# Key and query latents normed for all tokens at once, with the norm weights applied after the transposes, in a hybrid SSM and attention block

## The chip, the cores and the metric

The kernel runs on one core of a Trainium2 chip. The metric is device time in microseconds (us), the median of three runs. One further execution was recorded by the hardware profiler; every row shown here is from that execution.

## What is computed

One layer of a streaming encoder for 512 tokens of width 1024, all in float32. The part that the change touches is the projection of the normed input and the latent attention that follows it:

```python
h = rmsnorm(x, norm_mix_w)
u_ssd, u_mla = jnp.split(h @ w_in, [IN_SSD], axis=-1)
# u_ssd: gates z (1024), x (1024), B (512), C (512), dt (16)
y_ssd = ssd_mixer(u_ssd, ...)      # conv, SiLU, chunked scan, gate, grouped norm
q_lat, kv_lat, k_rope = jnp.split(u_mla, [384, 384 + 256], axis=-1)   # k_rope: 32
q  = rmsnorm(q_lat, q_norm_w) @ w_q_up        # 16 heads of 64 + 32
kv = rmsnorm(kv_lat, kv_norm_w) @ w_kv_up     # 16 heads of 64 + 64
# rotary embedding on q's last 32 columns and on k_rope, scale 96 ** -0.5,
# softmax over blocks of the past, y_mla = p @ v
x = x + concat([y_ssd, y_mla]) @ w_out
...  # memory attention, conv FFN, final norm
```

## The kernel before

Tokens stand in four tiles of 128 (`t` is a tile). A product in float32 is made of three matmuls on split operands (`mm3`, lines L103 to L105): each number is a high part (ScalarE, written ACT in the profile, copies it in a rounded type: L94, or with a scale per partition L98) and a low part (VectorE, written DVE, subtracts: L95, L99). Activations are split once. Weights come in **pages** (`wr`) of 128 partitions by 1024 numbers, loaded by SyncE's queue (SP) into three buffers and split into `wh` and `wl`, four buffers each. For each page ACT casts, then DVE subtracts (L95, whole page); while the flag `pool_helps` is set, DVE takes half (L157) and GpSimd (POOL) the other half (L158). The flag is set from the tenth of 16 steps of the state-space scan to the end of the memory attention.

The scan goes over four groups of heads with four chunks each. In groups 0 to 2 each step runs, ahead of its chunk, a **unit** of the next group's projections on TensorE (PE): B, C or one of two x units (`acc<-wh,Ah`, 24 matmuls of 256 or 512 columns), and a gate unit (`z_unit`), then `ssd_d`, `ssd_a`, `ssd_b` (the scan itself). An x unit is evicted through a convolution: ACT `cu`, three DVE passes (L434), DVE `cu` (L437), and four transposes (`tr<-cst,cu`). Group 3 has no next group; the table `PLAN` writes out what its four steps run. Its letters: `z` a gate unit; `l` a **late unit**, the last 432 of the latents' columns for one token tile (24 matmuls of 432 columns, four pages of 2x432); `d`, `a`, `b` the scan; `i` sets up tiles and weights of the latent norm; `q0` to `q3` and `k0` to `k3` norm the query and the key latents of one token tile; `p1` runs one out-projection part (`out_part`, 12 matmuls of 256 columns); `U` the first query up-projection (`q_up`, its rotary work on POOL, L726 to L729), `s` and `S` the setup of the key and query tiles.

`lat_norm` does per token tile: squares on ACT, mean and epsilon on DVE (`msl`, L140), the power -1/2 on POOL (`rsl`, L142), a multiplication by that and the weight row on DVE (L621), two or three transposes on PE (`tr<-cst,qkl`), and the splits on ACT and DVE for each 128x128 block (`lt`, L94, L95). `lat_kv` also turns `k_rope` on DVE (L635 to L638).

After group 3 comes the attention; it takes the remaining out parts, the second half of the out projection and the memory keys as fills, one or two a head. Memory attention and the feed-forward follow.

A scheduler orders each engine's queue from the program's text and its own estimates (except where `manual_schedule` fixes the first norm), and each engine works its queue strictly in order: an instruction that waits holds what stands behind it. At the start DVE and PE norm the token tiles one after the other: `ms` (L140), `xn` (L287), four transposes, the splits `Al`.

Of the kernel before, what the change touches and what calls it, by code (L numbers as in the profile page):

```python
# [7 lines left out]
F32 = mybir.dt.float32  # L8
# [6 lines left out]
P = 128  # L15
T = 512
# [17 lines left out]

PLAN = ('z z z z d a l l b', 'l l d a i q0 k0 p1 q1 b p1 q2 k1 p1 q3 k2', 'p1 d a k3 p1 b p1', 'p1 d U p2 b p3 s S')


def shape_constants():
    t = np.arange(P)[:, None]
    l = np.arange(P)[None, :]  # L40
    cen = ((t > 63) & (t <= l)).astype(np.float32) - ((t > l) & (t <= 63))
    c = np.concatenate([t == l, t <= l, cen, t <= l, t > l, np.ones((P, P))], axis=1).astype(np.float32)
    m = np.zeros((NT, 2, T), np.float32)
    for j in range(NT):
        m[j, 0, j * P:j * P + 64] = 1.0
        m[j, 1, j * P + 64:(j + 1) * P] = MASK_NEG
    f = np.array([np.float32(1.0) / np.float32(np.float64(10000.0) ** np.float64(np.float32(i) / np.float32(ROPE)))
                  for i in range(0, ROPE, 2)], np.float32).reshape(1, ROPE // 2)
    return c, m, f
# [13 lines left out]
def tile_block(ctx, tc, x, mem, positions, norm_mix_w, w_in, ssd_conv_w, ssd_conv_b, ssd_dt_bias,  # L63
# [80 lines left out]

    pool_helps = [False]
    def wload(src, a, b):
# [3 lines left out]

    def wsplit(raw, pool=False):
        _, a, b = raw.shape
        hi = base.tile([P, a, b], F32R, name="wh", tag="wh", bufs=4)
        lo = base.tile([P, a, b], F32R, name="wl", tag="wl", bufs=4)
        if pool or (pool_helps[0] and a > 1):
            nc.scalar.copy(hi, raw)  # L156
            nc.vector.tensor_tensor(lo[:, 0:a // 2], raw[:, 0:a // 2], f32(hi[:, 0:a // 2]), ALU.subtract)  # L157
            nc.gpsimd.tensor_tensor(lo[:, a // 2:], raw[:, a // 2:], f32(hi[:, a // 2:]), ALU.subtract)  # L158
        else:
            split(hi, lo, raw)  # L160
# [100 lines left out]
    ones = k1([1, P], "ones")  # L261
    nc.vector.memset(ones, 1.0)
    scb = base.tile([P, 16], F32, name="scb")
    drow = base.tile([P, SSD_H], F32, name="drow")
# [150 lines left out]
    nc.vector.tensor_copy(cosb[:, :, H2:], cosb[:, :, 0:H2])  # L415
    nc.vector.tensor_scalar(sinb[:, :, 0:H2], sinb[:, :, H2:], -1.0, None, ALU.mult)


# [186 lines left out]
    def lat_init():  # L605
        LT.extend(k4([P, 2, T], "lt", F32R) for _ in range(3))
        LT.extend(page("lt") for _ in range(2))
        qkl = k4([P, 1024], "qkl")
        box["qw"], box["kvw"] = row_tile(qkl[:, 0:QR], mla_q_norm_w), row_tile(qkl[:, QR:QR + KVR], mla_kv_norm_w)
        box["ln"] = qkl[:, QR + KVR:]  # L610
        nc.vector.tensor_scalar(box["qw"], box["qw"], float(QH) ** -0.5, None, ALU.mult)
        x4 = k4([P, 4, 256], "xo")
        xo.extend(x4[:, i] for i in range(3))
        box["lnk"] = [gw[0], x4[:, 3]]

    def lat_norm(t, o, n, w, l0, l1, ln):
        ss = small([P, 1], "ssl", 2)
        src = lat[:, t, SSD_H + o:SSD_H + o + n]
        nc.scalar.activation(ln, src, AF.Square, accum_out=ss)
        rs = rstd_of(ss, n, "l")  # L620
        nc.vector.scalar_tensor_tensor(ln, src, rs, w, ALU.mult, ALU.mult)  # L621
        ps = tr_bank().rearrange("p (k t) -> p k t", k=4)
        for k in range(l0, l1):
            transpose(ps[:, k - l0], ln[:, tsl(k - l0)])
        for k in range(l0, l1):
            split(LT[k][:, 0, tsl(t)], LT[k][:, 1, tsl(t)], ps[:, k - l0])

    def lat_q(t):
        lat_norm(t, 0, QR, box["qw"], 0, 3, box["ln"])

    def lat_kv(t):
        lat_norm(t, QR, KVR, box["kvw"], 3, 5, box["lnk"][t % 2])
        kr = lat[:, t, SSD_H + QR + KVR:]
        tmp = small([P, ROPE], "krt", 1)
        nc.vector.tensor_tensor(tmp[:, 0:H2], kr[:, H2:], sinb[:, t, 0:H2], ALU.mult)  # L635
        nc.vector.tensor_tensor(tmp[:, H2:], kr[:, 0:H2], sinb[:, t, H2:], ALU.mult)
        nc.vector.tensor_tensor(kr, kr, cosb[:, t], ALU.mult)
        nc.vector.tensor_tensor(kr, kr, tmp, ALU.add)  # L638

    with tc.issue_after(last):  # L640
# [24 lines left out]
    def late_unit(t):  # L665
# [5 lines left out]
        for k in range(KD):  # L671
            hi, lo = late_pages[k // 2]
            mm3(acc, (hT[0][:, k, tsl(t)], hT[1][:, k, tsl(t)]), (hi[:, k % 2], lo[:, k % 2]), k == 0, k == KD - 1)
        nc.scalar.copy(lat[:, t, 256:], acc)

    late = [lambda t=t: late_unit(t) for t in range(NT)]
# [8 lines left out]
    def setup_kq1():  # L685
        for b in range(2):
            kt = k4([P, 2, T], f"kt{b}", F32R)
            qt = k4([P, 2, T], f"qt{b}", F32R)
            for i, (tl, w) in enumerate(((qt, masks[:, 0]), (kt, masks[:, 1]))):
                nc.vector.memset(f32(tl[QH:KROWS, 1]), 0.0)  # L690
                nc.gpsimd.dma_start(tl[QH:KROWS, 0], w)
            kts.append(kt)
# [144 lines left out]
    def do(op, i):  # L837
# [11 lines left out]
        elif op == "i":  # L849
            lat_init()  # L850
        elif op[0] == "q":
            lat_q(int(op[1]))
        elif op[0] == "k":
            lat_kv(int(op[1]))
        elif op[0] == "p":
# [9 lines left out]
    for i, (g, c) in enumerate(seq):  # L865
        pool_helps[0] = i > 9
        if g + 1 < SSD_G:
# [180 lines left out]
    with tc.manual_schedule(engines={E_.PE, E_.Activation, E_.DVE}):  # L1048
# [47 lines left out]
        for n0 in (0, 256):  # L1096
            for m in range(2):
                fm_pass(accs0[m], pg0, m, h3t, n0, n0 + 256)
            if n0 == 0:
                scaled(3)  # L1100
                turn(3)
                store(3)
    pool_helps[0] = False
    acts = []
# [122 lines left out]
```

## Time and profile before

| | us |
|---|---|
| median of three runs | 987.85 (987.63 to 988.17) |
| the profiled execution, its own time | 987.27 |
| its span in the trace | 985.5 |
| PE busy in the span | 965.7 (98%) |
| DVE, ACT, POOL busy | 662.1 (67%), 523.4 (53%), 279.6 (28%) |

The span is what the trace covers; 1.8 us of the execution lie outside it. Busy times are sums over instructions of an engine; PE is the only engine near its span, so a time is read as PE's work plus the pauses in which PE waited.

### The profile page before, as it was taken

What the parts mean: (1) busy time and instruction counts of PE and PEld (TensorE: products, weight loads), DVE (VectorE), ACT (ScalarE), POOL (GpSimd) and SP (SyncE); (2) the same over time, 40 slices, a digit from 0 to 9 for tenths busy, and PEclk for the clock granted to TensorE, in tenths of its full rate; (3) what the DMA queues carried; (4) which work ended last, traced back from release to release, by engine and by line L of the source; (5) the groups of instructions that cost most, each with busy time, mean ns of one, the idle gap of its engine ahead of it and who ended that gap; (6) DMA issues with size and microseconds to landing.
All of it is one profiled execution on the core that took longest, in us unless ns stands there. A gap on an engine that the chain in (4) does not pass through costs nothing.

```text
span 985.5 us, 14980 instructions
## 1 busy us (share of the span) xinstructions
PE 965.7 (98%) x5385; PEld 843.0 (86%) x5385; DVE 662.1 (67%) x1210; ACT 523.4 (53%) x1078; POOL 279.6 (28%) x360
## 2 busy tenths in 40 slices
PE   8999999999999999999999999999999999999997
PEld 6889998898899999988888888888888888888886
DVE  5989999868779786773654435766667666722553
ACT  5677776655477677753544434444444444321442
POOL 2016547656653547452443222000000000000000
PEclk9999999999999999999999999999999999999999
DMA  7653432315423336242241120433223322332462
GB/s 242 208 175 95 116 108 77 97 49 179 155 78 103 113 113 233 86 155 80 86 150 65 65 86 22 128 107 107 86 87 108 105 85 93 113 116 97 156 223 80
DMA packets 90306, 114.07 MB, mean 116 GB/s; under 512 B 5799, under 2 KB 70119, under 8 KB 89848
## 3 DMA queue, kind: packets, MB, share of 16 engines
q1 hardware_dynamic: 88536, 106.78, 34.0%
q0 software_dynamic: 1696, 6.33, 2.1%
q8 instruction: 43, 0.70, 0.3%
q14 instruction: 31, 0.25, 0.1%
HBM read 104.67 MB, written 8.42 MB: 115 GB/s over the span
## 4 chain that ended last, share of the span: by engine, by line
PE 82%; DVE 7%; DMA 3%; ACT 3%; POOL 2%; issue 2%; SPq 0%; POOLq 0%; ACTq 0%; DVEq 0%
PE acc L103 22%; PE acc L105 22%; PE acc L104 22%; PE tr L119 3%; PE s L103 3%; PE s L105 3%; PE s L104 3%; PE pv L811 2%; DMA aE<-acT 2%; DVE wl L157 1%; ACT aE L544 1%; PE acc L119 1%; DVE cu L434 1%; DMA wr<-in_w_in_dram 1%; POOL xdD L550 1%
## 5 line engine op out<-in xcount | busy, mean ns | idle before, releaser
L103 PE MATMUL acc<-Ah,wh 128*128 128x512 f32 (+1 forms) x560 | 215.5, 385 | 0.2 <-ACT Ah L94 0.2
L104 PE MATMUL acc<-Al,wh 128*128 128x512 f32 (+1 forms) x560 | 215.4, 385 | 0.2 <-DVE Al L95 0.2
L105 PE MATMUL acc<-Ah,wl 128*128 128x512 f32 (+1 forms) x560 | 215.0, 384 | 0.0
L95 DVE TENSOR_TENSOR wl<-wr,wh 128x1024 fp32r<-128x1024 f32 (+1 forms) x99 | 120.0, 1213 | 101.6 <-ACT wh L94 100.9
L94 ACT CAST wh<-wr 128x1024 fp32r<-128x1024 f32 (+1 forms) x99 | 102.0, 1031 | 133.5 <-PE acc L104 63.7
L158 POOL TENSOR_TENSOR wl<-wr,wh 128x512 fp32r<-128x512 f32 (+2 forms) x64 | 103.5, 1625 | 86.2 <-ACT wh L156 79.8
L142 POOL TENSOR_TENSOR rs<-ms,neg_half 128x1 f32<-128x1 f32 x18 | 10.8, 600 | 409.5 <-DVE ms L140 397.9
L104 PEld LDWEIGHTS acc<-Al,wh 128*128 128x128 f32 x560 | 105.3, 188 | 20.3 <-DVE Al L95 0.5
L105 PEld LDWEIGHTS acc<-Ah,wl 128*128 128x128 f32 x560 | 105.3, 188 | 20.2
L103 PEld LDWEIGHTS acc<-Ah,wh 128*128 128x128 f32 x560 | 105.2, 188 | 20.0 <-ACT Ah L94 0.5
L156 ACT CAST wh<-wr 128x1024 fp32r<-128x1024 f32 (+2 forms) x64 | 65.4, 1029 | 40.1 <-PE s L105 10.7
L1121 DVE SCALAR_TENSOR_TENSOR cbuf<-acc,fcw,cbuf 128x511 f32<-128x511 f32 (+1 forms) x88 | 65.6, 747 | 26.6 <-ACT cbuf L1119 25.1
L157 DVE TENSOR_TENSOR wl<-wr,wh 128x512 fp32r<-128x512 f32 (+2 forms) x64 | 59.3, 932 | 35.7 <-ACT wh L156 34.7
L103 PE MATMUL acc<-wh,Ah 128*128 128x256 f32 (+2 forms) x240 | 77.2, 323 | 1.0 <-ACT Ah L94 1.0
L105 PE MATMUL acc<-wh,Al 128*128 128x256 f32 (+2 forms) x240 | 76.2, 319 | 0.0
L104 PE MATMUL acc<-wl,Ah 128*128 128x256 f32 (+2 forms) x240 | 75.9, 318 | 0.0
L795 POOL TENSOR_SCALAR p<-p,ri 128x128 f32<-128x128 f32 (+1 forms) x64 | 34.5, 542 | 71.7 <-DVE ri L794 71.1
L103 PEld LDWEIGHTS acc<-wh,Ah 128*128 128x128 f32 x240 | 46.1, 192 | 4.2 <-ACT Ah L94 1.4
L105 PEld LDWEIGHTS acc<-wh,Al 128*128 128x128 f32 x240 | 46.1, 192 | 2.6 <-DVE Al L95 0.3
L104 PEld LDWEIGHTS acc<-wl,Ah 128*128 128x128 f32 x240 | 46.2, 192 | 2.3
L1119 ACT ACTIVATE cbuf<-acc,fcb,fcw 128x512 f32<-128x512 f32 x44 | 34.3, 779 | 24.0 <-PE acc L105 24.0
L104 PE MATMUL acc<-wl,act 128*128 128x512 f32 (+1 forms) x112 | 40.5, 363 | 0.0
(370 smaller groups left out, 2349.3 us busy)
## 6 DMA issues: line engine op xcount, KB each, us to landing
wr<-in_w_ffn_up_dram SPq DMA_DIRECT2D x44, 512.0 KB, 3.5
wr<-in_w_ffn_down_dram SPq DMA_DIRECT2D x33, 512.0 KB, 3.3
wr<-in_w_in_dram SPq DMA_DIRECT2D x26, 512.0 KB, 3.9
wr<-in_w_out_dram SPq DMA_DIRECT2D x16, 512.0 KB, 3.5
aE<-acT POOLq DMA_DIRECT2D x16, 256.0 KB, 3.5
wr<-in_w_mem_k_dram SPq DMA_DIRECT2D x8, 512.0 KB, 4.5
wr<-in_w_mem_v_dram SPq DMA_DIRECT2D x8, 512.0 KB, 3.4
wr<-in_w_mem_q_dram SPq DMA_DIRECT2D x8, 512.0 KB, 3.6
```

Source lines behind the costliest of these rows:

```text
L94: first = nc.scalar.copy(hi, src)
L95: nc.vector.tensor_tensor(lo, src, f32(hi), ALU.subtract)
L103: nc.tensor.matmul(acc, lhsT=lh, rhs=rh, start=first, stop=False)
L104: nc.tensor.matmul(acc, lhsT=lh, rhs=rl, start=False, stop=False)
L105: nc.tensor.matmul(acc, lhsT=ll, rhs=rh, start=False, stop=last)
L119: nc.tensor.transpose(dst, src, ident[:n, :n])
L156: nc.scalar.copy(hi, raw)
L157: nc.vector.tensor_tensor(lo[:, 0:a // 2], raw[:, 0:a // 2], f32(hi[:, 0:a // 2]), ALU.subtract)
L158: nc.gpsimd.tensor_tensor(lo[:, a // 2:], raw[:, a // 2:], f32(hi[:, a // 2:]), ALU.subtract)
L795: nc.gpsimd.tensor_scalar(p_, p_, ri, 1.0, ALU.mult, ALU.mult)
L1119: nc.scalar.activation(u, acc, AF.Identity, scale=fcw[:, 2, m:m + 1], bias=fcb[:, m:m + 1])
L1121: nc.vector.scalar_tensor_tensor(u[:, s:], acc[:, :T - s], fcw[:, 2 - s, m:m + 1], u[:, s:], ALU.mult, ALU.add)
```

## The change

The norm of the latents is done once for all four token tiles (`n`): squares on ACT behind each late unit, one power on POOL for 128x8 sums, eight scalings on ACT in place, rotary work on DVE for all tiles at once. The norm weights are no longer rows that DVE multiplies by; they are loaded as columns (`latw`, weight by partition) and applied where the transposes are split (`t0` to `t4`, one bank of four transposes each). In group 3 the late units come first and the gate units after them; out parts in group 3 are ten instead of twelve. Weight pages, apart from the first two, are no longer halved with POOL. The mask tiles are loaded whole instead of half loaded and half set to zero. A DMA scratch size is set.

```diff
-PLAN = ('z z z z d a l l b', 'l l d a i q0 k0 p1 q1 b p1 q2 k1 p1 q3 k2', 'p1 d a k3 p1 b p1', 'p1 d U p2 b p3 s S')
+PLAN = ('d a l l l l n z b z', 'z z d a i b p1 t0 p1 t1', 'd a p1 t2 t3 b p1 t4 p1', 'd U p2 b p3 s S')
...
-    m = np.zeros((NT, 2, T), np.float32)
+    m = np.zeros((NT, 2, 2, T), np.float32)
...
-    def wsplit(raw, pool=False):
+    def wsplit(raw, halves=False):
...
-        if pool or (pool_helps[0] and a > 1):
+        if halves:
...
+    latw = base.tile([P, 64], F32, name="latw")
...
+    nc.sync.dma_start(latw[:, 0:3], mla_q_norm_w[0].rearrange("(k p) -> p k", p=P))
+    nc.sync.dma_start(latw[:, 3:5], mla_kv_norm_w[0].rearrange("(k p) -> p k", p=P))
+    nc.vector.tensor_scalar(latw[:, 0:3], latw[:, 0:3], float(QH) ** -0.5, None, ALU.mult)
...
-        qkl = k4([P, 1024], "qkl")
-        box["qw"], box["kvw"] = row_tile(qkl[:, 0:QR], mla_q_norm_w), row_tile(qkl[:, QR:QR + KVR], mla_kv_norm_w)
...
-        nc.scalar.activation(ln, src, AF.Square, accum_out=ss)
-        rs = rstd_of(ss, n, "l")
-        nc.vector.scalar_tensor_tensor(ln, src, rs, w, ALU.mult, ALU.mult)
...
-            split(LT[k][:, 0, tsl(t)], LT[k][:, 1, tsl(t)], ps[:, k - l0])
...
+    def lat_norm():
...
+        rs = small([P, 2 * NT], "lrs", 1)
+        for i, n in enumerate((QR, KVR)):
+            h = slice(i * NT, (i + 1) * NT)
+            nc.vector.tensor_scalar(lss[:, h], lss[:, h], 1.0 / n, EPS, ALU.mult, ALU.add)
+        nc.gpsimd.tensor_tensor(rs, lss, neg_half.broadcast_to([P, 2 * NT]), ALU.pow)
+        for t in range(NT):
+            for i, (o, n) in enumerate(((SSD_H, QR), (SSD_H + QR, KVR))):
+                v = lat[:, t, o:o + n]
+                nc.scalar.activation(v, v, AF.Copy, scale=rs[:, i * NT + t:i * NT + t + 1])
+        kr = lat[:, :, SSD_H + QR + KVR:]
+        tmp = small([P, NT, ROPE], "krt", 1)
+        nc.vector.tensor_tensor(tmp[:, :, 0:H2], kr[:, :, H2:], sinb[:, :, 0:H2], ALU.mult)
...
+    def lat_T(k):
+        ps = tr_bank()
+        for t in range(NT):
+            transpose(ps[:, tsl(t)], lat[:, t, SSD_H + P * k:SSD_H + P * (k + 1)])
+        split(LT[k][:, 0], LT[k][:, 1], ps, latw[:, k:k + 1])
...
+        for i, (o, m) in enumerate(((SSD_H, QR), (SSD_H + QR, KVR))):
+            nc.scalar.activation(acc[:, 0:m], lat[:, t, o:o + m], AF.Square, accum_out=lss[:, i * NT + t:i * NT + t + 1])
...
-            for i, (tl, w) in enumerate(((qt, masks[:, 0]), (kt, masks[:, 1]))):
-                nc.vector.memset(f32(tl[QH:KROWS, 1]), 0.0)
-                nc.gpsimd.dma_start(tl[QH:KROWS, 0], w)
+            for i, tl in enumerate((qt, kt)):
+                nc.gpsimd.dma_start(tl[QH:KROWS], masks[:, i])
...
-        pool_helps[0] = i > 9
...
-    nc = _bacc.Bacc("TRN2", target_bir_lowering=False, num_devices=1)
+    nc = _bacc.Bacc("TRN2", target_bir_lowering=False, num_devices=1, dynamic_dma_scratch_size=8192)
```

Three places of the queues, before and now. First, DVE at the start of the program, where the second and third token tiles are normed (`ms`, `xn`). Before:

```order
L157 TENSOR_TENSOR wl<-wr,wh 128x512 x2
L95 TENSOR_TENSOR Al<-tr,Ah 128x4x128 x2
L140 TENSOR_SCALAR ms<-ss 128x1 x2
L287 SCALAR_TENSOR_TENSOR xn<-x,rs,s 128x512 x2
L95 TENSOR_TENSOR Al<-pv,Ah 128x4x128
```

Now:

```order
L156 TENSOR_TENSOR wl<-wr,wh 128x512 x2
L95 TENSOR_TENSOR Al<-tr,Ah 128x4x128 x2
L140 TENSOR_SCALAR ms<-ss 128x1
L421 TENSOR_SCALAR latw<-latw 128x3
L140 TENSOR_SCALAR ms<-ss 128x1
L287 SCALAR_TENSOR_TENSOR xn<-x,rs,s 128x512 x2
```

The scaling of the latent weights, which stands far down in the text, is queued between two steps of the first norm, and waits there for a load. That load's place in SP's queue now:

```order
L259 DMA cst<-in_consts_dram 128x128
L319 DMA drow<-in_ssd_d_dram 128x16
L419 DMA latw<-in_mla_q_norm_w_dram 128x3x1
L420 DMA latw<-in_mla_kv_norm_w_dram 128x2x1
L147 DMA wr<-in_w_in_dram 128x8x128
```

It stands right behind `drow` and ahead of the first page of the B unit, which followed `drow` before.

Second, POOL at the end of the scan, around the latent norm's power (`rsl`; `rsy` and `y` belong to the scan's own norm, `qrow` and `rt` to the queries' rotary work). Before:

```order
L142 TENSOR_TENSOR rsl<-msl,neg_half 128x1 x2
L593 TENSOR_TENSOR y<-y,gw 128x256
L142 TENSOR_TENSOR rsy<-msy,neg_half 128x1
L726 TENSOR_TENSOR rt<-qrow,sinb 128x4x16
L727 TENSOR_TENSOR rt<-qrow,sinb 128x4x16
L593 TENSOR_TENSOR y<-y,gw 128x256
L728 TENSOR_TENSOR qrow<-qrow,cosb 128x4x32
L567 TENSOR_TENSOR xdD<-xdD,y_478 128x256
L729 TENSOR_TENSOR qrow<-qrow,rt 128x4x32
L142 TENSOR_TENSOR rsl<-msl,neg_half 128x1 x2
```

Now, where the one power (`lrs`) stands:

```order
L555 TENSOR_TENSOR xdD<-xrow,dt 128x256
L556 TENSOR_TENSOR xdD<-xdD,dec 128x256
L581 TENSOR_TENSOR S<-S,dec 128x256
L624 TENSOR_TENSOR lrs<-lss,neg_half 128x8
L555 TENSOR_TENSOR xdD<-xrow,dt 128x256
```

The power has moved from behind the queries' rotary work to a place ahead of the last three chunks' outputs, and the rotary work now follows everything of the scan.

Third, DVE around the last x unit (group 3's second, whose convolution is L434 before, L439 now) and the late pages (`wl` 128x432 halves before, 128x864 whole now). Before:

```order
L95 TENSOR_TENSOR M<-aE,M 128x512
L586 TENSOR_TENSOR y<-pv,xdD 128x256
L157 TENSOR_TENSOR wl<-wr,wh 128x512
L577 TENSOR_TENSOR S<-s,S 128x256
L587 TENSOR_TENSOR y<-pv,y 128x256
L588 SCALAR_TENSOR_TENSOR y<-y,zrow 128x256
L95 TENSOR_TENSOR S<-S 128x256
L140 TENSOR_SCALAR msy<-ssy 128x1
L157 TENSOR_TENSOR wl<-wr,wh 128x512
L434 SCALAR_TENSOR_TENSOR cu<-acc,scw,cu 128x511
```

Now, the second, third and fourth late pages with what stands between them:

```order
L95 TENSOR_TENSOR wl<-wr,wh 128x864
L439 SCALAR_TENSOR_TENSOR cu<-acc,scw,cu 128x511
L140 TENSOR_SCALAR msy<-ssy 128x1
L439 SCALAR_TENSOR_TENSOR cu<-acc,scw,cu 128x510
L546 TENSOR_TENSOR cbm<-s,cst 128x128
L439 SCALAR_TENSOR_TENSOR cu<-acc,scw,cu 128x509
L95 TENSOR_TENSOR Bl<-tr,Bh 128x2x128
L551 TENSOR_TENSOR aE<-aE,cbm 128x512
L571 TENSOR_TENSOR y_482<-s,dec 128x256
L95 TENSOR_TENSOR wl<-wr,wh 128x864
L524 SCALAR_TENSOR_TENSOR zrow<-zrow,acc 128x256
L95 TENSOR_TENSOR wl<-wr,wh 128x864
```

Ahead of the first of these rows stand, in order, the first late page, `M`, `S`, two `y`, `S` and `y` of the scan. The late pages have moved ahead, between the last two chunks of group 2.

## Rows read from the trace of the kernel before

**Rows 1.** Windows: start to end, length, then busy time (count) of each engine, PE clock, DMA.

```profile
0.00:20.00 20.00, 15.08 (x73) 11.54 (x74) 9.41 (x20) 11.34 (x20) 5.96 (x10) 1.00 0.87 276
...
180.00:260.00 80.00, 73.76 (x493) 69.68 (x493) 60.56 (x143) 44.68 (x118) 52.83 (x70) 0.96 0.38 117
260.00:480.00 220.00, 219.67 (x1447) 202.28 (x1447) 158.14 (x368) 144.67 (x369) 100.60 (x145) 1.00 0.37 121
```

**Rows 2.** Waits of PE from 140 to 300 us, the three largest.

```profile
PE tr L119 <- DVE lt L95: 2.1, 1, 2.1
PE tr L119 <- DVE cu L437: 1.4, 1, 1.4
PE s L103 <- DVE cbm L541: 1.2, 1, 1.2
```

**Rows 3.** Windows of 5 us with a lowered PE clock, columns as above.

```profile
225.00:230.00 5.00, 4.82 (x29) 4.61 (x28) 5.00 (x16) 2.69 (x9) 1.58 (x2) 0.66 0.79 249
...
250.00:255.00 5.00, 5.00 (x28) 5.00 (x29) 3.99 (x12) 1.99 (x6) 3.85 (x8) 0.66 0.12 33
```

**Rows 4.** POOL's timeline before the first wait: start, duration, instruction, idle before.

```profile
246.65 0.45 POOL L729 TENSOR_TENSOR qrow<-qrow,rt 128x128 f32<-128x128 f32 x1
247.06 1.05 POOL L142 TENSOR_TENSOR rsl<-msl,neg_half 128x1 f32<-128x1 f32 x2
```

**Rows 5.** DVE's timeline before the three waits.

```profile
187.79 1.54 DVE L157 TENSOR_TENSOR wl<-wr,wh 128x432 fp32r<-128x432 f32 x1
...
221.08 2.99 DVE L157 TENSOR_TENSOR wl<-wr,wh 128x512 fp32r<-128x512 f32 x2 [0.26 <-ACT wh L156]
...
247.64 0.62 DVE L621 SCALAR_TENSOR_TENSOR qkl<-lat,rsl,qkl 128x384 f32<-128x384 f32 x1 [2.17 <-POOL rsl L142]
```

**Rows 6.** DVE's groups by form: count, busy us, mean ns of one, idle before.

```profile
L95 DVE TENSOR_TENSOR wl<-wr,wh 128x1024 fp32r<-128x1024 f32 x95 | 116.6, 1229 | 101.1 <-ACT wh L94 100.6
L157 DVE TENSOR_TENSOR wl<-wr,wh 128x512 fp32r<-128x512 f32 x56 | 51.8, 930 | 34.1 <-ACT wh L156 33.1 <-PE acc L104 0.7
...
L546 DVE TENSOR_TENSOR aE<-aE,cbm 128x512 f32<-128x512 f32 x16 | 13.1, 816 | 0.0
L95 DVE TENSOR_TENSOR M<-aE,M 128x512 fp32r<-128x512 f32 x16 | 12.9, 804 | 0.4 <-ACT M L94 0.4
...
L99 DVE SCALAR_TENSOR_TENSOR mq<-acc,mq 128x512 fp32r<-128x512 f32 x8 | 5.5, 686 | 4.1 <-ACT mq L98 4.1
```

**Rows 7.** A window ahead of the late units, columns as in rows 1.

```profile
150.00:180.00 30.00, 29.00 (x181) 25.53 (x180) 29.05 (x54) 21.72 (x51) 20.85 (x26) 1.00 0.19 56
```

**Rows 8.** DVE's timeline around the last x unit.

```profile
177.70 1.23 DVE L95 TENSOR_TENSOR M<-aE,M 128x512 fp32r<-128x512 f32 x1
...
184.42 2.32 DVE L434 SCALAR_TENSOR_TENSOR cu<-acc,scw,cu 128x511 f32<-128x511 f32 x3
```

**Rows 9.** PE's timeline: first matmul of that x unit, and two of a late unit.

```profile
178.79 0.28 PE L103 MATMUL acc<-wh,Ah 128*128 128x256 f32 x1
...
200.13 0.36 PE L104 MATMUL acc<-wl,Ah 128*128 128x432 f32 x1
200.33 0.36 PE L105 MATMUL acc<-wh,Al 128*128 128x432 f32 x1
```

**Rows 10.** SP's timeline: issue of `drow`.

```profile
5.84 0.59 SPq L319 DMA_DIRECT2D drow<-in_ssd_d_dram  x1
```

**Rows 11.** Tile `drow`: issue to landing of its load.

```profile
DMA to landing us min/median/max: 7.7/7.7/7.7
```

**Rows 12.** Tile `rot`: issue to landing of the positions, 512 single numbers, issued at 19.63.

```profile
DMA to landing us min/median/max: 2.1/2.1/2.1
```

**Rows 13.** DVE's timeline at the second tile's norm, and PE's first transposes of it.

```profile
12.96 0.15 DVE L140 TENSOR_SCALAR ms<-ss 128x1 f32<-128x1 f32 x1 [0.88 <-ACT xn L281]
13.04 1.41 DVE L287 SCALAR_TENSOR_TENSOR xn<-x,rs,s 128x512 f32<-128x512 f32 x2
...
13.94 1.06 PE L119 MATMUL pv<-cst,xn 128*128 128x128 f32 x4 [0.18 <-DVE xn L287]
```

More of the change, by code (lines that the diff above doesn't have):

```diff
@@ L42, in shape_constants @@
     c = np.concatenate([t == l, t <= l, cen, t <= l, t > l, np.ones((P, P))], axis=1).astype(np.float32)
-    m = np.zeros((NT, 2, T), np.float32)
+    m = np.zeros((NT, 2, 2, T), np.float32)
     for j in range(NT):
-        m[j, 0, j * P:j * P + 64] = 1.0
-        m[j, 1, j * P + 64:(j + 1) * P] = MASK_NEG
+        m[j, 0, 0, j * P:j * P + 64] = 1.0
+        m[j, 1, 0, j * P + 64:(j + 1) * P] = MASK_NEG
     f = np.array([np.float32(1.0) / np.float32(np.float64(10000.0) ** np.float64(np.float32(i) / np.float32(ROPE)))
@@ L143, in rstd_of @@
         return rs
-    pool_helps = [False]
     def wload(src, a, b):
@@ L607, in lat_init @@
         LT.extend(page("lt") for _ in range(2))
-        qkl = k4([P, 1024], "qkl")
-        box["qw"], box["kvw"] = row_tile(qkl[:, 0:QR], mla_q_norm_w), row_tile(qkl[:, QR:QR + KVR], mla_kv_norm_w)
-        box["ln"] = qkl[:, QR + KVR:]
-        nc.vector.tensor_scalar(box["qw"], box["qw"], float(QH) ** -0.5, None, ALU.mult)
         x4 = k4([P, 4, 256], "xo")
[L613 to L618, printed above, removed]
-        nc.scalar.activation(ln, src, AF.Square, accum_out=ss)
-        rs = rstd_of(ss, n, "l")
-        nc.vector.scalar_tensor_tensor(ln, src, rs, w, ALU.mult, ALU.mult)
[L622 to L625, printed above, removed]
-            split(LT[k][:, 0, tsl(t)], LT[k][:, 1, tsl(t)], ps[:, k - l0])
@@ L628, in lat_q @@
[L628 to L637, printed above, removed]
-        nc.vector.tensor_tensor(kr, kr, tmp, ALU.add)
+        xo.extend(x4[:, i] for i in range(4))
@@ new lines, in tile_block @@
+    lss = small([P, 2 * NT], "lss", 1)
+    def lat_norm():
[11 more added lines that the diff above has]
+        nc.vector.tensor_tensor(tmp[:, :, 0:H2], kr[:, :, H2:], sinb[:, :, 0:H2], ALU.mult)
+        nc.vector.tensor_tensor(tmp[:, :, H2:], kr[:, :, 0:H2], sinb[:, :, H2:], ALU.mult)
+        nc.vector.tensor_tensor(kr, kr, cosb, ALU.mult)
+        nc.vector.tensor_tensor(kr, kr, tmp, ALU.add)
@@ L850, in do @@
             lat_init()
[L851 to L854, printed above, removed]
+        elif op == "n":
+            lat_norm()
+        elif op[0] == "t":
+            lat_T(int(op[1]))
         elif op[0] == "p":
@@ L1102, in tile_block @@
                 store(3)
-    pool_helps[0] = False
     acts = []
```

## The prediction

> **What bounds the kernel now.** I read the windows of the whole span first, to see in which stages PE, the engine with 98% of the span, has room to gain anything. From 260 to 480 us, where the attention runs, PE is busy for 219.67 of 220 us. From 180 to 260 us, where group 3's scan, the late units, the latent norm and the first out parts run, it is busy for 73.76 of 80: 6.2 us of pauses, at a mean clock of 0.96 [rows 1]. So the stage that the change rewrites is the one in which PE waits, and only what moves PE there, or at the start, can move the time. From 0 to 20 us PE has 4.9 us of pauses, with the DMA engines 87% busy [rows 1].
>
> Then the list of PE's waits for 140 to 300 us: three are long. Transposes of a normed latent wait 2.1 us for DVE's `lt`, transposes of an x unit 1.4 us for `cu`, and a matmul of the scan 1.2 us, behind which the mask product `cbm` had not been made [rows 2]. Together 4.7 of the 6.2 us; the rest is in shorter waits.
>
> Then windows of 5 us, for the clock. It is 0.66 in the window behind the `cbm` wait and in the one behind the `lt` wait [rows 3], and full elsewhere. A mean of 0.66 over 5 us costs (1 - 0.66) x 5 = 1.7 us, twice 3.4 us. Behind the 1.4 us wait no window shows a lowered clock, so a pause near this length costs its own length, or that plus 1.7. The stage thus loses 6.2 + 3.4 = 9.6 us.
>
> Last, the timelines of the two engines that PE waits for. At 247.64 us DVE multiplies a query latent by its norm, after 2.17 us idle for `rsl` [rows 5]; POOL began that power at 247.06, right behind the rotary work of the query up-projection [rows 4]. Small norm steps stood in POOL's queue behind work that nobody needed yet. The other two waits are pages: DVE's half of a late page took 1.54 us at 187.79, two halves took 2.99 us at 221.08 [rows 5], against 0.93 us for one in the mean [rows 6], so `cu` and `cbm` came late behind them in DVE's queue.
>
> **What the change removes.** The query and key norms become one `n`. Its power stands ahead of the rotary work in POOL's queue, its eight scalings on ACT, and between the last late unit and the first transpose of a latent PE has 96 matmuls of gate units and three out parts of 12: the spacing of 0.20 us for 432 columns [rows 9] gives 0.12 for 256, so 132 x 0.12 = 15.8 us. The chain that must fit in there is two small DVE steps, a power of the kind that took 0.5 us [rows 4] and eight scalings; even at 0.7 us each, the price of a 512 wide pass [rows 6], they take 5.6 us, in all some 7. So the 2.1 us wait goes, and its clock loss of 1.7 with it. The 20 small `lt` splits become five wide ones at 0.69 us, by the nearest form [rows 6].
>
> The pages are no longer halved, so the stretched halves ahead of `cu` and `cbm` are gone, and POOL no longer works beside DVE on them. A whole page costs DVE 1.23 us instead of 0.93 [rows 6]; about ten pages lie in this stage, so 3 us more DVE work, covered by 19 us of idle DVE there [rows 1], to which the norm's multiplications, most of the rotary work and the memsets add what they took. The convolution's result is needed by transposes that now stand inside the second late unit, late enough. I take both waits as gone, 1.4 + 1.2, with the clock loss of 1.7 behind the second. In the attention the same costs DVE some 7 us in 220, of which it leaves 62 idle [rows 1]; no price.
>
> Removed: 2.1 + 1.4 + 1.2 + 3.4 = **8.1 us**. The lower bound is the 3.8 us of the latent norm alone, the upper one all 9.6.
>
> **What it adds: the first late unit.** The late units now come right behind group 2's last x unit. DVE has no room there: 29.05 of 30 us busy from 150 to 180 us [rows 7]. Call the x unit's start X, 178.79 in this trace [rows 9]. PE needs the third late page after 24 matmuls of 0.12 (2.9), some 19 small ones for the scan at no more than 0.12 (2.3) and 12 matmuls of 0.20 (2.4): X + 7.6. DVE's queue until that page's low half, in the order shown above: `M` started at 177.70, X - 1.1 [rows 8]; the first late page comes ahead of it (864/1024 of 1.23, 1.04), so `M` starts at X. Then `M` 0.8, five steps half or less as wide at 0.4 (2.0), the second page 1.04, the convolution 2.32 [rows 8], three small ones and `msy` 1.2, `aE` 0.8, the third page 1.04: 9.2, so X + 9.2. PE pauses 1.6 us; I take **1.7**, since the fourth page is two steps further. Bounds: nothing, if the scheduler's order leaves DVE earlier than X; 4 us, if two pages stretch as the one at 187.79 did. As the row of the clock shows one loss in two pauses of 1.2 to 1.4 us, half of 1.7 goes with it, **0.85**.
>
> **What it adds: the start.** The scaling of `latw` stands in DVE's queue between two `ms`, ahead of the second tile's `xn`, and waits for a load that SP issues right behind `drow`. `drow` is issued at 5.84, takes 0.59 of SP [rows 10] and lands 7.7 us after issue [rows 11], though it has only 8 KB: the queues are full of the first pages. With the same 7.7, `latw` lands at 6.43 + 7.7 = 14.1 us. DVE would then scale, do `ms` and start `xn` at 14.4, where it now starts it at 13.04, right behind `ms` at 12.96. PE already waits 0.18 us for that `xn` [rows 13], so all of the delay of 1.4 us is a pause of PE: **1.4** (0.6, if the load travels a little faster, to 2.0). A clock loss behind it is again not excluded, from 0 to 1.7; half, **0.85**. The two issues delay SP's next page by 0.6 us each; that page's DVE split comes five or more steps later, behind all of the first norm, which hides it.
>
> The load is of single numbers, 384 and 256 of them. The Trainium skill, "DMA: Bandwidth & Descriptors", section "Rules for kernel authors", says that a last dimension which is not contiguous lowers to one descriptor per element and should be rearranged; by that rule this form of load is the worst choice. The row nearest to it is the load of the positions, 512 single numbers: 2.1 us with the queues nearly idle [rows 12], so that form by itself has no price beyond what the queue gives.
>
> **Sum.** 8.1 removed, 1.7 + 0.85 + 1.4 + 0.85 = 4.8 added: 3.3 us less. Against the profiled execution's own 987.27 that is 984.0. The median before is 0.58 above that execution, so the forecast is **984.5 us** as a median.
>
> **The rivals.**
>
> *The load at the start comes in time* (17%). If `latw` takes 2.1 us, as the positions did [rows 12], it lands at 8.5, four us ahead of `ms`, and DVE does not stop. Against it stands `drow`, issued 0.6 us earlier. The time would be 984.5 - 2.25 = 982.3. The Trainium skill, same page, section "Latency and other measured facts", gives tiny transfers a round trip of about 0.8 us and memory access up to 2 us at high load; by it the load would land near 9, which is this rival. `drow`'s 7.7 us disagrees with it here.
>
> *No change* (21%). All of groups 1 to 3 is dealt anew, and a queue that works strictly in order finds new places to wait. One new pause of 1.6 us, of the length of the `cu` and `cbm` waits [rows 2], and one clock loss, 1.6 + 1.7 = 3.3, eat what the sum leaves: 987.8. For it speaks that before, with every page halved, DVE was full ahead of this stage [rows 7] and that long pauses stood in three unrelated places; against it that DVE and POOL both have less to do.
>
> *Slower* (16%): the gate units starve. Late pages hold all four `wh` and `wl` buffers until the last late unit frees them, so the two gate pages can be split only during that unit. It lasts 24 x 0.20 = 4.8 us, and two whole subtractions of 1.23 [rows 6] fit behind their casts, if DVE is free then. It has `xs`, `M` and `y` steps of two chunks in its queue near there, 0.8 us each. From a pause of 3.6 us at this place on, with one clock loss of 1.7, the sum is over 989.8. With six such steps late, 4.8 us, and the two subtractions behind them, 2.5, the pause is 7.3 less the 1.4 us that PE needs for the first page's matmuls, 5.9; with the clock loss 7.6: 992.1.
>
> The forecast itself has 46%.
>
> **How the numbers follow.** About 0.2%, 2 us, is what a measurement of this kernel can tell from no change: faster is below 985.9, slower above 989.8. The forecast's own range, with the pause of the late unit between 0 and 4 and the start between 0.6 and 3.7, is 982 to 987; a sixth of it lies within 0.2%. So faster: 0.46 x 5/6 + 0.17 + a little of *no change* = 0.57. Same: 0.27. Slower: 0.16. The range of 8 in 10 reaches from 980, where the first late unit costs nothing either and the start little, to 990, where half of the slower cases lie outside.
>
> **What would show it.** In the profile after: no wait of a transpose for `lt` near the latent norm, and no window of 0.66 behind one; a wait of DVE for `latw` near 12 to 14 us, and PE's transposes of the second tile at 15.3 instead of 13.94; a wait of PE for a late page of 1 to 2 us near 185; the attention still with under 1 us of pauses. The prediction is wrong if the start shows no such wait, if gate or out-part pages come late (waits for `wl` of several us between 200 and 230), or if lowered clocks appear in more windows than before.

## The result, and the profile after

The changed kernel takes 998.16 us (median of four runs, 994.85 to 999.68), the kernel before beside it 987.91: a ratio of 1.0099 [1.0074, 1.0125]. It is slower by about 10 us, and outside the predicted range of 980 to 990. The profiled execution took 997.91, with a span of 996.1 us, 10.6 more than before. PE is busy for 2.4 us more with the same 5385 matmuls, so the other 8.2 are pauses:

```profile
PE 968.1 (97%) x5385; PEld 844.2 (85%) x5385; DVE 660.7 (66%) x1165; ACT 525.4 (53%) x1071; POOL 184.5 (19%) x291
```

The windows of the changed kernel, in the stages used ahead of the prediction and the two that follow (columns as in [rows 1]):

```profile
0.00:20.00 20.00, 14.37 (x50) 10.82 (x51) 9.02 (x19) 9.87 (x17) 5.32 (x9) 1.00 0.89 277
180.00:260.00 80.00, 74.97 (x532) 71.34 (x531) 57.40 (x115) 52.81 (x125) 40.44 (x58) 1.00 0.41 126
260.00:490.00 230.00, 223.78 (x1442) 204.50 (x1441) 161.41 (x363) 143.34 (x364) 61.00 (x117) 0.99 0.35 114
490.00:660.00 170.00, 167.56 (x869) 141.44 (x868) 95.42 (x159) 73.63 (x157) 10.40 (x22) 1.00 0.28 90
385.00:390.00 5.00, 3.57 (x15) 3.47 (x16) 0.84 (x4) 0.98 (x5) 1.25 (x2) 0.51 1.02 381
390.00:395.00 5.00, 5.00 (x33) 4.73 (x32) 4.36 (x11) 3.61 (x11) 1.44 (x3) 0.81 0.08 29
```

The same two later stages of the kernel before:

```profile
260.00:490.00 230.00, 229.67 (x1499) 210.77 (x1499) 167.04 (x379) 151.95 (x382) 107.87 (x151) 1.00 0.37 121
490.00:660.00 170.00, 169.49 (x872) 143.33 (x871) 92.19 (x162) 72.97 (x156) 40.08 (x40) 1.00 0.29 90
```

From 180 to 260 us the change did in part what it was made for: PE idles 5.0 us instead of 6.2 [rows 1], at full clock, so 1.2 us of pauses and the 3.4 us of [rows 3] came back (from 140 to 180 us it idles 1.9 instead of 1.0). But in the attention PE now idles 6.2 us where it idled 0.3, with two windows of lowered clock, (1 - 0.51) x 5 + (1 - 0.81) x 5 = 3.4 us; and from 490 us on 2.4 us instead of 0.5. Most of the time was lost where the prediction had put no term. The list of PE's waits over the whole span says for what (engine and line, who was waited for, us in total, times, longest):

```profile
PE tr L119 <- POOL y L598: 4.7, 5, 1.9
PE acc L103 <- DMA memT<-memT_d: 2.4, 1, 2.4
PE acc L103 <- ACT Ah L94: 2.4, 3, 1.1
...
PE tr L119 <- DVE lt L99: 1.6, 3, 0.9
...
PE acc L104 <- DVE Al L95: 0.9, 1, 0.9
```

`cu` and `cbm` of [rows 2] are gone. `lt` is 1.6 us in three waits instead of 2.1 in one. `y` of the scan has grown from 0.6 us to 4.7. `memT` is new, and so are, behind 490 us, 1.3 of the 2.4 us for `Ah` and the 0.9 for `Al`, in the memory norm; the rest of `Ah` is at the start, as before.

**The memory load.** `memT`, the transposed memory, is loaded into the buffer that holds the scan's output `yS`, so it can be loaded only when the last out part has read that. PE's timeline of the kernel before, from the last matmul of an out part to the first that reads `memT`:

```profile
365.25 0.28 PE L105 MATMUL acc<-wh,Bl 128*128 128x256 f32 x1
...
366.28 0.42 PE L103 MATMUL acc<-wh,lt 128*128 128x384 f32 x1
...
375.45 0.34 PE L105 MATMUL acc<-wh,lt 128*128 128x384 f32 x1
...
375.85 0.36 PE L103 MATMUL acc<-memT,wh 128*128 128x256 f32 x1
...
376.39 0.28 PE L104 MATMUL acc<-memT,wh 128*128 128x256 f32 x1
```

and of the changed kernel:

```profile
377.46 0.28 PE L105 MATMUL acc<-wh,Bl 128*128 128x256 f32 x1
...
383.46 0.39 PE L786 MATMUL s<-kt,qt 100*128 100x256 f32 x1 [0.99 <-ACT p L795]
...
386.43 0.79 PE L103 MATMUL acc<-memT,wh 128*128 128x256 f32 x2 [2.40 <-DMA memT<-memT_d]
```

Before, the last query up-projection (`acc<-wh,lt`, 36 matmuls of 384 columns) stood in those 10.6 us, and the load landed in them. In the changed kernel there are 10 out parts in group 3 instead of 12, so the attention has two more to run; every later fill moves back by two places, and the last out part falls behind that up-projection. What is left between takes PE some 5 us. The load comes in two halves, issued on POOL's queue, high parts first; the first half landed after 7.7 us, at 386.4, and released the waiting matmul:

```profile
378.70 1.17 POOL L830 DMA_DIRECT2D memT<-memT_d  x2
```

```profile
DMA to landing us min/median/max: 7.7/9.3/10.9
```

That half also took longer: 7.7 us here, 5.7 in the kernel before. An estimate from these rows: with 5.7 us it would have landed at 384.4, and PE had run out of other work at 384.03. So only some 0.4 of the 2.40 us would be left without the slower load. Of all kernels in this document, the first half took 7.1 to 9.0 us in the four whose PE waits for `memT`, and 5.6 to 6.0 in the ten where it does not. Why it is slower at that place no run tests.

The pauses at `memT` are 0.26 + 0.99 + 2.40 us (the first for `p` at 381.13). Another 1.9 us of the attention's 6.2 stand in the first heads, where the kernel before has 0.2:

```profile
270.86 0.52 PE L119 MATMUL tr<-cst,p 128*128 128x128 f32 x3 [0.73 <-DVE PT L95]
...
300.65 1.25 PE L814 MATMUL pv<-PT,v 128*128 128x512 f32 x7 [0.66 <-DVE PT L95]
...
307.38 0.84 PE L814 MATMUL pv<-PT,v 128*128 128x512 f32 x3 [0.48 <-DVE PT L95]
```

**The start.** DVE's timeline of the changed kernel shows the wait that was forecast, 1.66 us for `latw`, whose load of 1.5 KB was issued at 6.81 and landed 6.8 us later. PE's first transposes of the second tile began at 14.64 (13.94 before, [rows 13]). The matmuls behind them follow each other every 0.21 us up to 19.79, and every 0.12 from then on; before, they did so from 15.4 on. The profile's clock column gives 1.00 for both, so this half pace is read from the spacing alone. DVE's timeline, then PE's:

```profile
11.80 0.15 DVE L140 TENSOR_SCALAR ms<-ss 128x1 f32<-128x1 f32 x1
13.61 0.17 DVE L421 TENSOR_SCALAR latw<-latw 128x3 f32<-128x3 f32 x1 [1.66 <-DMA latw<-in_mla_q_norm_w_dram]
13.69 0.14 DVE L140 TENSOR_SCALAR ms<-ss 128x1 f32<-128x1 f32 x1
13.75 1.40 DVE L287 SCALAR_TENSOR_TENSOR xn<-x,rs,s 128x512 f32<-128x512 f32 x2
```

```profile
14.64 1.09 PE L119 MATMUL pv<-cst,xn 128*128 128x128 f32 x4 [0.89 <-DVE xn L287]
...
19.37 0.41 PE L105 MATMUL acc<-wh,Al 128*128 128x256 f32 x1
19.58 0.41 PE L103 MATMUL acc<-wh,Ah 128*128 128x256 f32 x1
...
20.07 0.28 PE L103 MATMUL acc<-wh,Ah 128*128 128x256 f32 x1
20.19 0.28 PE L104 MATMUL acc<-wl,Ah 128*128 128x256 f32 x1
```

**The memory norm.** In the changed kernel the last transposes of the normed tokens stand directly ahead of the query matmuls that need them:

```profile
506.18 1.03 PE L119 MATMUL s<-cst,xn 128*128 128x128 f32 x8
508.23 0.73 PE L103 MATMUL acc<-Ah,wh 128*128 128x512 f32 x2 [1.02 <-ACT Ah L94]
509.82 0.50 PE L104 MATMUL acc<-Al,wh 128*128 128x512 f32 x1 [0.86 <-DVE Al L95]
```

Before, 13 matmuls of the memory values stood between, 496.07 to 499.13 us, and the splits were done during them.

### The profile page after: what moved, and what is told of

Its sections match the earlier page's. It is cut to its first block, busy times and chain, and to the rows that moved or that the text cites. A ratio compares the mean times of both kernels' runs of the same rounds, so it can differ in the third digit from the quotient of the medians.

```text
span 996.1 us, 14835 instructions
## 1 busy us (share of the span) xinstructions
PE 968.1 (97%) x5385; PEld 844.2 (85%) x5385; DVE 660.7 (66%) x1165; ACT 525.4 (53%) x1071; POOL 184.5 (19%) x291
## 4 chain that ended last, share of the span: by engine, by line
PE 79%; DVE 7%; DMA 5%; ACT 3%; POOL 3%; issue 2%; SPq 1%; POOLq 0%; ACTq 0%; DVEq 0%
PE acc L103 22%; PE acc L104 21%; PE acc L105 21%; PE tr L119 3%; PE s L103 2%; PE s L104 2%; PE s L105 2%; DMA aE<-acT 2%; PE pv L814 2%; DVE wl L95 1%; DMA memT<-memT_d 1%; ACT aE L549 1%; DMA latw<-in_mla_q_norm_w_dram 1%; PE pv L588 1%; PE acc L119 1%
## 5 line engine op out<-in xcount | busy, mean ns | idle before, releaser
L95 DVE TENSOR_TENSOR wl<-wr,wh 128x1024 fp32r<-128x1024 f32 (+3 forms) x161 | 194.0, 1207 | 135.4 <-ACT wh L94 132.1
L94 ACT CAST wh<-wr 128x1024 fp32r<-128x1024 f32 (+3 forms) x161 | 165.4, 1030 | 167.4 <-PE acc L104 73.3
L103 PE MATMUL acc<-wh,act 128*128 128x512 f32 (+1 forms) x112 | 40.5, 363 | 0.0
L105 PE MATMUL acc<-wh,act 128*128 128x512 f32 (+1 forms) x112 | 40.4, 363 | 0.0
L103 PE MATMUL acc<-wh,Bh 128*128 128x256 f32 x128 | 37.8, 295 | 0.0
```

Source lines behind the costliest of these rows:

```text
L94: first = nc.scalar.copy(hi, src)
L95: nc.vector.tensor_tensor(lo, src, f32(hi), ALU.subtract)
L103: nc.tensor.matmul(acc, lhsT=lh, rhs=rh, start=first, stop=False)
L105: nc.tensor.matmul(acc, lhsT=ll, rhs=rh, start=False, stop=last)
```

## The experiments

Every run is compared with the kernel before on the same chip; its median moved from 987.1 to 988.0 from chip to chip, so ratios are compared, and 0.001 is 1 us.

**Twelve parts.**

```diff
-PLAN = (..., 'd U p2 b p3 s S')
+PLAN = (..., 'd U p2 b p5 s S')
```

> The changed kernel, with the last step of group 3 running five out parts instead of three, so that twelve parts stand there as before. Theory: the ten parts of the change push the last out part two fills back, past the query up-projection (36 matmuls of 384 columns) that stood between it and the first memory key unit, so memT's load is no longer covered (pauses of 0.26 + 0.99 + 2.40 us before and at the first memT matmul, then two windows at 0.51 and 0.81 of the clock, 2.45 + 0.95 us). With the cover back these 7 us go: 990 to 992 us. Rival, that memT is late because its load is slower or because whole pages keep DVE and ACT late in the attention: no change, 996 to 1000.

989.30 us, ratio 1.0016 [1.0005, 1.0027]: 8 us of the 10 come back with this edit, as the theory of the cover said, a little more. The load is as long as in the kernel before, 5.7 to 9.2 us, and hidden: the first matmul with `memT` is at 376.00, 10.35 us behind the last out part, without a wait. So the rival's slower load belongs to the other place too; it is not a matter of pages or scratch. The waits of the first heads are gone as well (0.2 us left), which the theory did not have. The waits behind 490 us stay.

**More fills, ten parts.**

```diff
-        return int(i < 0 or qi == 1 or (qi == 0 and i > 3))
+        return int(i < 0 or qi == 1 or (qi == 0 and i > 1))
```

> The changed kernel with ten out parts in group 3 as it is, but with a second fill per head from head 2 on instead of head 4. The last out part then comes back ahead of the last query up-projection without a change in group 3. Theory of the cover: 990 to 992 us, as with twelve parts. If the number of parts in group 3 matters by itself (PE work there that hides page splits), only the twelve part version gains and this one stays at 996 to 1000.

991.63 us, 1.0052 [1.0040, 1.0064]. The wait for `memT` is gone with ten parts too, so it is the place of the load and not the number of parts in group 3 that makes it. 3.6 us less came back than with twelve parts. Of this 1.6 us are waits of 0.41, 0.85 and 0.37 us for DVE and ACT between 270 and 311 us, in the first heads. The changed kernel has 1.9 us there without the additional fills, and its version with twelve parts 0.2. So the number of parts in group 3 does matter there, ahead of the first heads, as the second half of the expectation allowed; where the other 2 us are is open.

**The kernel before, ten parts.**

```diff
-PLAN = (..., 'p1 d U p2 b p3 s S')
+PLAN = (..., 'p1 d U p2 b p1 s S')
```

> The kernel before with one edit: three instead of five out parts behind the scan of group 3's last step count two less (ten in all), norms, pages, masks and late units as before. Theory of the cover: memT's first use is again right behind the last out part, and the kernel before loses what the changed one loses there: 987.9 + 5 to 7 = 993 to 995 us. Rival, that slower pages or the smaller scratch make memT late: 987 to 989.

999.23 us, 1.0126 [1.0113, 1.0139]: two parts fewer cost the kernel before 12 us, more than the whole change does. Its PE timeline and clock:

```profile
310.49 0.39 PE L103 MATMUL s<-kt,qt 100*128 100x256 f32 x1 [1.57 <-ACT p L792]
...
388.18 0.33 PE L119 MATMUL tr<-cst,p 128*128 128x128 f32 x1 [0.97 <-POOL p L795]
393.58 0.80 PE L103 MATMUL acc<-memT,wh 128*128 128x256 f32 x2 [3.48 <-DMA memT<-memT_d]
```

```profile
390.00:395.00 5.00, 1.52 (x7) 1.41 (x7) 1.14 (x3) 0.94 (x3) 0.00 (x0) 0.71 1.05 379
395.00:400.00 5.00, 5.00 (x24) 4.76 (x23) 3.38 (x10) 3.16 (x9) 0.91 (x3) 0.61 0.31 110
```

At `memT` it loses 0.38 + 0.97 + 3.48 us and 3.4 us of clock, 8.2 in all; some 4 us more in waits between 266 and 313 us (1.20, 0.50, 0.50, 1.57, 0.35), in the first heads, as in the two other kernels with ten parts above. The number of fills in these heads is the same; what is missing is two parts of PE's work ahead of them. The expectation had the place of `memT` right and missed this second part. Pages and scratch, the rival, are those of before here and play no part.

**The factor in the norm.**

```diff
-    nc.vector.tensor_scalar(latw[:, 0:3], latw[:, 0:3], float(QH) ** -0.5, None, ALU.mult)
...
-            nc.vector.tensor_scalar(lss[:, h], lss[:, h], 1.0 / n, EPS, ALU.mult, ALU.add)
+            f = 1.0 if i else float(QH)
+            nc.vector.tensor_scalar(lss[:, h], lss[:, h], f / n, f * EPS, ALU.mult, ALU.add)
```

> The changed kernel without DVE's scaling of latw at the start; the factor 96 ** -0.5 is taken into the mean and epsilon of the query norm, so DVE's queue no longer holds a step that waits for latw there, and all other queues are the same. Theory: the start loses 2.3 us by that wait (0.7 us more pauses and 1.5 us more at half pace between 10 and 20 us), which come back: 995.5 to 996.5. Rival, that the second tile's norm is late for the two extra loads in SP's queue and not for the wait: no change, 998.

995.29 us, 1.0089 [1.0075, 1.0103]: 2.9 us by the medians, but only 1.0 by the ratios, whose intervals overlap. The trace tells it better. The first `cu` transposes, those of the first unit behind the start, come at 52.64, 52.01, 52.79 and 52.55 us in the four kernels that scale `latw` at the start, and at 50.07 to 51.52, in the mean 50.7, in the ten that do not (the kernel before among them): 1.8 us for the wait and its half pace, each from one profiled execution of a kernel.

**Halves kept.**

```diff
-        if halves:
+        if halves or (pool_helps[0] and a > 1):
...
+        pool_helps[0] = i > 9
...
+    pool_helps[0] = False
```

> The changed kernel with pages halved between DVE and POOL again, from the tenth step of the scan to the memory attention as before; all else as changed. Theory: whole pages cost time, for with them the queues put the last token tile's transposes of the memory norm behind all memory value matmuls (with halves 16 of these stand between), and PE waits 1.0 + 0.9 us there with a lowered clock behind; the waits of the scan's transposes for POOL's y (4.7 us) also stand behind whole pages in DVE's queue. Both back: 998 - 2 to 998 - 5 = 993 to 996 us, memT still uncovered. Rival, the prediction's own: halves stretch DVE, and bringing them back brings back the waits for cu and cbm with their clock, some 4 us: 999 to 1003.

996.52 us, 1.0095 [1.0081, 1.0108], against 1.0099 of the change: no difference that can be told. (The flag `i > 9`, with i from 0, is set from the eleventh step on.) Both theories have a part: the waits behind 490 us are gone (169.49 us busy of 170) and those for `y` fall from 4.7 to 1.4 us, but 1.1 us for `zrow` is new in group 3, and the wait for `memT` is longer (3.81 us, the first half landing after 9.0).

**The kernel before, whole pages.**

```diff
-        pool_helps[0] = i > 9
```

> The kernel before without the halving (the flag is never set), all else as before; ten steps of its table untouched, memT covered. Theory that whole pages cost time by themselves: the memory norm's wait of 1.3 to 1.9 us with its clock appears and y waits appear, 989 to 992 us. Rival, the prediction's own step: the waits for cu and cbm and their clock loss go, 983 to 985.

985.31 us, 0.9972 [0.9961, 0.9983]. My theory that whole pages cost time fell; the prediction's own step holds. The windows:

```profile
180.00:260.00 80.00, 78.14 (x565) 75.06 (x564) 66.68 (x158) 49.72 (x128) 40.96 (x63) 1.00 0.44 139
490.00:660.00 170.00, 167.72 (x850) 141.00 (x850) 91.98 (x154) 69.71 (x149) 9.77 (x20) 0.99 0.25 82
```

In group 3 PE idles 1.9 us instead of 6.2 and the clock stays up: the waits for `cu` and `cbm` went with the halves alone, with the latent norm as it was, and in place of the 2.1 us for `lt` stand three of 0.75, 0.59 and 0.26 us near the norm, without a clock loss. And the memory norm's waits came (2.3 us idle behind 490 us).

**Twelve parts and the factor.** The edits of the first and fourth experiment together.

> The changed kernel with twelve out parts in group 3 and with the query factor taken into the norm, so with both losses found so far undone. If they are independent, their differences to the changed kernel add: 998.2 - 8.9 - 2.9 = 986.4 us; if the start's delay was hidden in later waits of the longer kernel, it stays near 989.

986.81 us, 0.9999 [0.9989, 1.0008]: 1.7 us below twelve parts alone. With these two undone no cost or gain of the change can be told.

**Twelve parts, the factor, halves.** The same with the edit of the fifth experiment.

> As the version with twelve parts and the factor in the norm, and with halved pages as before, which leaves the norm for all tokens at once, the table's order with late units first, and the masks. Theory that whole pages cost 2 to 4 us: 982.5 to 984.5 us, faster than both kernels. Rival, halves stretch DVE beside POOL and the waits for cu and cbm come back: 987 to 990.

987.33 us, 0.9996 [0.9986, 1.0006]. The time is the rival's, in part by other waits than it named: the memory norm's wait is gone, and in group 3 stand 1.12 us for `zrow` and 1.44 for `xo`, with 0.43 for `cu`. Against 0.9999 without halves no difference can be told.

**Gate units first.**

```diff
-PLAN = ('d a l l l l n z b z', 'z z d a i b p1 t0 p1 t1', ...)
+PLAN = ('z z z z d a l l b', 'l l n d a i b p1 t0 p1 t1', ...)
```

> The version with twelve parts and the factor in the norm, whole pages, with the gate units put back ahead of the late units in group 3's table (the first two steps read: four gate units, d, a, two late units, b; two late units, n, d, a, i, b, p1, t0, p1, t1). Theory: late units first put the scan's d and a of group 3 right at the step's start, so ACT stands waiting for the load of aE with the scaling of y queued behind it, and PE waits 0.89 + 1.01 + 1.89 us for y, with 1.0 us of clock behind; gate units first gives these back: 986.8 - 3.5 to - 4.8 = 982 to 983.5 us. Rival: the y waits come from the norm at once (its squares and scalings on ACT) or from whole pages, wherever the late units stand: 986 to 988.

991.11 us, 1.0030 [1.0019, 1.0040]: slower by 3 us than with late units first, so this theory fell. Of the waits for `y` the longest is gone and two remain (0.89 and 1.19 us), and a new one of 2.35 us for the scan's `S` came. The cause shows in the next kernel but one, which has the same table.

**The kernel before, whole pages to the attention.**

```diff
-        pool_helps[0] = i > 9
...
+    pool_helps[0] = True
     for u in fills:
         u()
```

> The kernel before with whole pages through the scan and the attention and halves only from the end of the attention to the memory attention. Theory: whole pages gave 2.2 us in sum because they take away 4.4 us of pauses and the clock losses in group 3 and add a wait in the memory norm (1.29 + 0.43 us, one clock loss of 1.7), where the last token's transposes stand behind all memory value matmuls; with halves there the order is as before and that wait goes: 985.3 - 3.4 = 982 us (981 to 983). Rival, that the lateness there is handed on from the attention and not made by the order: 985.

980.00 us, 0.9923 [0.9911, 0.9936]: by the ratios 7.6 us faster than the kernel before and 17 faster than the changed one, and 4.8 us below whole pages everywhere. Group 3 and the memory norm both run without waits of over 0.6 us:

```profile
180.00:260.00 80.00, 78.68 (x561) 75.91 (x560) 64.87 (x157) 49.54 (x127) 42.48 (x64) 0.98 0.45 137
490.00:660.00 170.00, 169.50 (x867) 143.33 (x866) 91.56 (x158) 72.62 (x152) 39.29 (x38) 1.00 0.28 87
```

**Gate units first, halves late.** The edits of the last two experiments on the changed kernel with twelve parts and the factor.

> The version with twelve parts, the factor in the norm and gate units first, with halves only from the end of the attention to the memory attention. If the theories of order, whole pages and memory norm all hold, the gains add to that of gate units first: 983 - 3.4 = 979 to 981 us, faster than both kernels and at or below the kernel before with whole pages to the attention. If the norm for all tokens at once gives nothing by itself, it equals that one, 982. Rival, y waits stay: 984 to 986.

986.55 us, 0.9986 [0.9977, 0.9994]: 4.4 us below gate units first, again the price of the memory norm, and far from 980. ACT's timeline in group 3, and PE's:

```profile
228.64 3.73 ACT L629 ACTIVATE lat<-lat,lrs 128x384 f32<-128x384 f32 x8 [1.34 <-POOL lrs L625]
232.28 0.39 ACT L94 CAST S<-S 128x256 fp32r<-128x256 f32 x1
```

```profile
236.04 0.56 PE L103 MATMUL s<-S,bc 128*128 128x256 f32 x1 [2.34 <-ACT S L94]
```

The eight scalings are one block of 3.73 us in ACT's queue, behind 1.34 us idle for the power; the scan's `S` stands behind the block, its next steps on POOL and DVE follow late, and PE waits 2.34 us for the `S` of the next chunk. This chain is read from the trace; no run takes the scalings out of that place.

**The change with its three losses undone.** Late units first, the norm at once; twelve parts, the factor, and halves only from the end of the attention.

> The changed kernel's own table (late units first) and its norm for all tokens at once, with the three losses found undone: twelve parts in group 3, the factor in the norm, and halves from the end of the attention to the memory attention. If the memory norm's loss adds as it did in the two kernels where halves came back there (5.3 and 4.6 us), it is 986.8 - 5 = 981 to 982.5 us. Against the kernel before with whole pages to the attention (980.0) the rest is then what the late units first and the norm at once cost or give by themselves: 1 to 2.5 us more, by the waits for y of 3.8 us against 1.2. Rival, that they gain once the losses are gone, as the prediction had it: below 980.

983.98 us, 0.9964 [0.9950, 0.9978]: 3.5 us below the version without the late halves, and 3.6 us below the kernel before. Against whole pages on the kernel before (0.9923) it is 4.1 us slower: PE still waits for `y`, 0.89 + 0.90 + 1.53 us from 172 to 204, and for `lt` 0.93. The 4.1 us are what everything else in the change costs together: the norm at once, the late units first, the whole mask tiles, the scratch size and the loads of `latw`. No run separates these.

## Why the prediction was wrong

The three undone losses are 8.2 us (1.0099 to 1.0016, parts), 1.7 (to 0.9999, start) and 3.5 (to 0.9964, memory norm), 13.4 together, and the change without them gains 3.6: +9.8. That this adds up is no proof, since each is taken behind the one before; alone on the changed kernel the factor gave 1.0 by the ratios.

*The step that failed* is the premise that "only what moves PE there, or at the start, can move the time", "there" being group 3. From it follow "In the attention the same costs DVE some 7 us in 220, of which it leaves 62 idle [rows 1]; no price" and "the attention still with under 1 us of pauses" at the end. It looked at how busy the attention is and not at the order in it: a stage without pauses can still be given some. The two out parts fewer have no term in the sum. The runs show 6.2 us of pauses in the attention and 3.4 of clock in their place. Two parts fewer moved the load of `memT` off its cover (3.65 us of pauses and the 3.4 of clock) and left the first heads short of work ahead of them (1.9 us). Putting them back gave 8.2 us. For `memT` it is shown by undoing it, by getting the cover back another way, and by making the same loss in the kernel before; the waits of the first heads go with the number of parts in the same runs.

The warning stood in the trace of the kernel before. POOL issued the two halves of `memT` at 365.7 and 366.4. The second landed 9.4 us later, at 375.8, and is first read at 376.39; the first had landed 5.7 us after its issue, 4.4 us before its first use at 375.85:

```profile
365.71 1.21 POOL L827 DMA_DIRECT2D memT<-memT_d  x2 [3.78 <-PE s L784]
```

```profile
DMA to landing us min/median/max: 5.7/7.5/9.4
```

*Not in the sum at all* was the memory norm either. Whole pages, far from where the change works, turn the order of transposes and matmuls there. In every kernel with halved pages there the matmuls of the memory values stand between and PE has no wait at this place; in every one with whole pages it waits 1.7 to 1.9 us. Halves from the attention's end on gave 3.5 to 4.8 us in three pairs of kernels; in two of the three pairs 1.7 us of clock went with the wait.

*The start* was right in mechanism and a little large: 1.4 + 0.85 forecast, 1.8 by the `cu` marker, 1.7 by the pair of runs. Of it only 0.7 us is the pause (the transposes of the second tile at 14.64, not 15.3), the rest the longer half pace. `latw` landed after 6.8 us, not 7.7. The Trainium skill, "DMA: Bandwidth & Descriptors", section "Latency and other measured facts", gives tiny transfers a round trip of no less than about 0.8 us and memory access 2 us at high load. An estimate from it, 2 us behind the issue at 6.81, is 8.8 us. The trace does not agree: the load landed at 13.6, in a stretch where the DMA engines are 89% busy. The neighbouring load `drow` (7.7 us) was the better guide.

*The terms for `cu` and `cbm`* were right, in mechanism too: whole pages alone took these waits and the clock loss away. *The `lt` wait* went only in part. Its clock loss is gone, but the forecast "no wait of a transpose for `lt`" did not hold: 0.93, 0.34 and 0.29 us remain, in the splits of the blocks and not in the norm, whose scalings are done by 226 us, ahead of the first transposes at 230.7. Whole pages alone bring it down as far, so the norm at once was not needed for it:

```profile
239.42 0.63 PE L119 MATMUL tr<-cst,lat 128*128 128x128 f32 x4 [0.93 <-DVE lt L99]
```

*The first late unit*, forecast as a pause of 1.7 us for a page, shows no wait for a page. In the same stage stand waits for `y`:

```profile
184.82 0.44 PE L119 MATMUL tr<-cst,y 128*128 128x128 f32 x2 [0.88 <-POOL y L598]
...
205.41 0.44 PE L119 MATMUL tr<-cst,y 128*128 128x128 f32 x2 [1.86 <-POOL y L598]
```

ACT's timeline in the changed kernel shows how the second is made:

```profile
200.10 1.28 ACT L549 ACTIVATE aE<-aE,cenT 128x128 f32<-128x128 f32 x4 [2.19 <-DMA aE<-acT]
...
202.96 0.51 ACT L597 ACTIVATE y<-y,rsy 128x256 f32<-128x256 f32 x1
```

ACT stood 2.2 us for a load of the next chunk, with the scaling of the finished `y` behind it. This was only read from the trace, and what makes the other waits for `y` no run shows. Gate units first removed this wait, left two shorter ones for `y` ahead of it and brought a dearer one, so what a better table would give stays open.

*The rival for slower*, gate pages that starve, did not happen: PE waits for no `wl` between 200 and 230 us. The kernel is slower by a mechanism that was not on the list.

## What to carry to other kernels

When work is moved out of a stage into fills elsewhere, follow the whole list of fills: a load into a reused buffer may have had its cover by the place of one fill. Look in the trace for loads that land just in time, and ask of each what stands between the last reader of its buffer and its first use, now and after. Ask also how long the load takes at its new place. And split a change into its parts on the chip early: here one part of it, whole pages, is worth 7.6 us on the kernel before if the halves are kept behind the attention, and the rest of the change together costs.

## What was not expected of the hardware

The power on 128x8 numbers took POOL 1.65 us in the gate-first kernel, three times that on 128x1 [rows 4], and 2.10 in the changed one. A load of 1.5 KB took 6.8 us at the start, and single loads of `memT` between 5.6 and 11.2 us from kernel to kernel. The clock fell behind some pauses of 1 to 2 us and not behind others of the same length, and in other places in different kernels. At the same place, behind a wait for `S` of 2.35 us, the windows of the gate-first kernel lose 3.4 us of clock (0.58 and 0.74 of 5 us each), and behind one of 2.34 us in the version with halves late 1.7 (0.66). Runs of one kernel spread over 1.6 to 6.3 us; what part of this is the clock was not tested.
